# The last down product by Strassen's seven products, with weight sums added up in DRAM by accumulating DMAs

## The chip, the core and the metric

The kernel runs on one core of one Trainium2 chip. The metric is the device time of one execution in microseconds (us). A core has TensorE (PE in the profile; its weight loads are PEld), VectorE (DVE), ScalarE (ACT), GpSimd (POOL) and SyncE (SP), each with an instruction queue of its own that it works through in order, and 16 DMA engines that carry every transfer.

## The reference, cut to what matters

Two transformer blocks run one after the other on 512 tokens of width 1024. The change is in the last matrix product of the second block.

```python
D_MODEL = 1024
SEQ = 512
D_FF_2 = 2816

def second_block(x, ...):
    ...
        x = x + rmsnorm(y @ w_out[l], g_post_mix[l])
        h = rmsnorm(x, g_pre_ffn[l])
        gu = h @ w_ffn_in[l]
        gate, up = gu[..., :D_FF_2], gu[..., D_FF_2:]
        x = x + rmsnorm((jax.nn.silu(gate) * up) @ w_ffn_down[l], g_post_ffn[l])
    return x
```

The last product multiplies the hidden rows (512 tokens x 2816) by `w_ffn_down` (2816 x 1024). Its result is normalized per token, scaled by a gain, added to x, and is the output.

## The kernel before

All arithmetic is float32 at near full accuracy: each operand is split into a high part (a rounding CAST on ACT, line 93) and a low part (the difference, on DVE, line 98), and each product is three matmuls, high by high, high by low and low by high (`mm3`, `mm3s`, issued on line 109). A 128x128 block is the stationary operand, and up to 512 columns move past it.

Weights come through one stream, `Stream`. `_dma` (line 166) loads a tile of 128 partitions x 1024 columns (512 KB) into one of six `raw` buffers from SP's queue; `_split` makes its high and low parts in tiles `q`, of which there are 39. `next(key)` hands out the next pair and keeps up to `AHEAD` = 4 tiles split in advance. The order of the stream is written out beforehand, in `second_order` for the second block.

The order of instructions on each engine is not that of the Python code: the tile framework's scheduler places each instruction in its engine's queue by its dependences. `keep_in_program_order` pins a few of them.

The up products (gate and up, class `UpPairs`) already use seven products per pair of hidden tiles. `out` and `out_plain` leave each of the 22 hidden tiles (128 hidden x 512 tokens) in half a `q` tile, `gt(f)`.

`ffn_out` computes the last product. For every hidden tile f it splits `g[f]` once and takes one weight tile of 128 x 1024. For each of four token tiles t and two halves of the columns c it adds three matmuls 128x512 into one of eight PSUM banks: 22 x 4 x 2 x 3 = 528 matmuls. The last six hidden tiles are done token tile by token tile, so that the norm and the output of one token tile lie beside the products of the next:

```python
            k.mm3(ps[t][c], g[f][:, 0, t * P : (t + 1) * P], g[f][:, 1, t * P : (t + 1) * P],
                  w[0][:, c * 512 : (c + 1) * 512], w[1][:, c * 512 : (c + 1) * 512], f == 0, f == NF - 1)
```

One place at the program's start matters too. The first feed-forward block's norm is taken late: PE begins with products of the unnormalized x, and while they run, the sums of squares go through DVE (`nv`, line 317), through a power of -0.5 on POOL (`nr`, line 325), which is POOL's first arithmetic, back to DVE (line 332, a diagonal tile `b`) and to PE, which spreads them over all partitions by `ones` matmuls. The rows of this broadcast stand in PE's queue between two groups of products:

```python
    k.nc.gpsimd.tensor_tensor(out, in_, k.mhalf[:, :w], op=ALU.pow)
```

Of the kernel before, what the change touches and what calls it, by code (L numbers as in the profile page):

```python
# [8 lines left out]
F32 = mybir.dt.float32  # L9
# [6 lines left out]
P = 128  # L16
# [20 lines left out]
class Ctx:  # L37
    def __init__(self, ctx, tc, aps):
        self.tc = tc
        self.nc = tc.nc  # L40
        self.a = aps
        pool = lambda name, bufs, **kw: ctx.enter_context(tc.tile_pool(name=name, bufs=bufs, **kw))
        self.cp = pool("cp", 1)
        self.rawp = pool("raw", Stream.RAW)
        self.qp = pool("q", 39)
        self.bp = pool("b", 8)
        self.sp = pool("sm", 4)
        self.psp = pool("ps", 8, space=bass.MemoryType.PSUM)
# [373 lines left out]
class UpPairs:  # L422
# [125 lines left out]
    def run(self):  # L548
# [9 lines left out]
        for n, num in steps:  # L558
# [25 lines left out]
            if (n, num) == (NF // 2 - 1, 7):  # L584
                for f in range(2):
                    split_g(k, self.g, f)
# [1319 lines left out]
def tile_block(ctx: ExitStack, tc: tile.TileContext, aps, out):  # L1906
# [37 lines left out]
    second_order(W, aps)  # L1944
# [37 lines left out]

    M = Mixer(k)
# [11 lines left out]
    cat = [None] * KD  # L1995
    tq, tk, tg = M.ret_specs(rb)
# [4 lines left out]
    M.gates()  # L2001
    mem1 = Memory(k, aps["memT"], G["norm_mem_kv"])
# [3 lines left out]
    del mem1  # L2006
    xs, norm = [], Norm(k)
# [8 lines left out]
    run_all(weave(MA.q_stack(0), u, RATES["mq"]) or ())  # L2016
    k2d = dr.tile([4, P, 256], F32, name="k2d")
# [24 lines left out]
    del mem2  # L2042
    ops, norm = Operands(k), Norm(k)
# [24 lines left out]
    run_all(second_mix(k, G, x, xs, norm, norm5, k2d, v2d, dr, out))  # L2068


def second_order(W, a):
# [36 lines left out]
    for f in range(NF):  # L2108
        W.add(("down", f), a["w_ffn_down"][f])


def second_mix(k, G, x, xs, norm, norm5, k2d, v2d, dr, out):
# [36 lines left out]
    ns = Nsa(k, rt, rb)  # L2149
    u = units(k, [("T", ("q2", h), take_q2) for h in range(4)] + [("R", ("mlv", 0), ml.take_v)], xs, first)  # L2150
# [106 lines left out]
    def resid(h):  # L2257
        last = pns[h].finish()
        return lambda: resid2(h, last())
# [62 lines left out]
    up = UpPairs(k, ("gate", "up"), ops, finish, 6, lambda: resid(1))  # L2322
    g = up.run()
    gb = k.q([P, 2, S])
    nc.sync.dma_start(gb, k.a["g_post_rows"])
    ffn_out(k, "down", g, xtd, gb, e2, out)


def ffn_out(k, key, g, xtd, gb, e2, out):

    nc = k.nc
    last = 6
    ps = [[k.ps(), k.ps()] for t in range(NT)]

    def chunk(t, f, w, cs=(0, 1)):
        for c in cs:
            k.mm3(ps[t][c], g[f][:, 0, t * P : (t + 1) * P], g[f][:, 1, t * P : (t + 1) * P],
                  w[0][:, c * 512 : (c + 1) * 512], w[1][:, c * 512 : (c + 1) * 512], f == 0, f == NF - 1)  # L2340

    split_g(k, g, 0)
    for f in range(NF - last):
        split_g(k, g, f + 1)
        w = k.W.next((key, f))
        for t in range(NT):
            chunk(t, f, w)
    for f in range(NF - last + 1, NF):
        split_g(k, g, f)
    xt = []  # L2350
    for t in range(NT):
        xt.append(k.q([P, 2, S]))
        nc.sync.dma_start(xt[t], xtd[t])
    ws = [k.W.next((key, f)) for f in range(NF - last, NF)]
    for t in range(NT):
        for cs in ((0, 1),) if t < NT - 1 else ((0,), (1,)):
            for j, w in enumerate(ws):
                chunk(t, NF - last + j, w, cs)
        ss = k.small([P, 2], "os")
        ys = []  # L2360
        for c in range(2):
            sq, y = k.b(), k.b()
            nc.scalar.activation(sq, ps[t][c], AF.Square, scale=D**-0.5, accum_out=ss[:, c : c + 1])
            nc.vector.tensor_mul(y, ps[t][c], gb[:, c, :])
            ys.append(y)
        v = k.small([P, 1], "ov")
        nc.vector.scalar_tensor_tensor(v, ss[:, 0:1], e2[:, t : t + 1], ss[:, 1:2], op0=ALU.add, op1=ALU.add)  # L2367
        r = k.small([P, 1], "or")
        k.rsqrt(r, v)
        for c, y in enumerate(ys):  # L2370
            nc.vector.scalar_tensor_tensor(y, y, r, xt[t][:, c, :], op0=ALU.mult, op1=ALU.add)
            (nc.sync, nc.scalar)[c].dma_start(out[t][:, c * 512 : (c + 1) * 512], y)
# [56 lines left out]
def _host(inputs):  # L2429
# [38 lines left out]
    o["w_ffn_down"] = i["w_ffn_down_2"][0].reshape(NF, P, D)  # L2468
# [47 lines left out]
```

## Time and profile before

| what | value |
|---|---|
| time, median of 3 runs | 2206.36 us (2205.94 to 2207.67) |
| time of the profiled execution | 2205.79 us |
| its span, first to last instruction | 2204.0 us |
| PE busy | 2180.3 us (99%) |
| DVE busy | 1519.0 us (69%) |
| ACT busy | 1021.3 us (46%) |
| POOL busy | 307.8 us (14%) |
| granted TensorE clock, mean | 0.999 |

The profiled execution takes 1.8 us more than its span, for what lies around the instructions. Busy time counts the time in which an engine has an instruction under way; matmuls overlap, so that a row's mean duration is longer than the distance from one to the next.

### The profile page before, as it was taken

The numbers are of one execution on the slowest core, as the hardware profiler recorded it, in microseconds if no ns is written. First come the engines' busy times: TensorE is split into PE (matmuls) and PEld (weight loads), VectorE is DVE, ScalarE is ACT, GpSimd is POOL, SyncE is SP. The second block draws the span as 40 slices with busy tenths as digits, with TensorE's granted clock in tenths as the row PEclk, the third lists the DMA queues.
The fourth block names the chain that finished last, engine by engine and source line by source line (L and its number), as shares of the span: only waits on it lengthen the run. The fifth ranks groups of instructions, "written<-read, shape, count | busy, mean of one in ns | idle before, by whom it ended". The sixth has DMA issues, their size and how long they took to land.

```text
span 2204.0 us, 32737 instructions
## 1 busy us (share of the span) xinstructions
PE 2180.3 (99%) x12746; PEld 1902.9 (86%) x12746; DVE 1519.0 (69%) x2605; ACT 1021.3 (46%) x1794; POOL 307.8 (14%) x363
## 2 busy tenths in 40 slices
PE   9999999999999999999999999999999999999998
PEld 8999888888888889999888878887787789999987
DVE  7888644656866667888445955836888757888832
ACT  6545523545344544456324543315667636454620
POOL 0000022301234030000240000313334200000000
PEclk9999999999999999999999999999999999999999
DMA  5233524212333332335134122531111453133521
GB/s 177 96 116 108 183 64 136 79 61 86 124 125 106 106 115 77 115 106 188 55 116 149 54 92 97 185 138 59 48 59 55 131 169 116 61 113 106 166 102 39
DMA packets 78627, 235.73 MB, mean 107 GB/s; under 512 B 9092, under 2 KB 13444, under 8 KB 78472
## 3 DMA queue, kind: packets, MB, share of 16 engines
q1 hardware_dynamic: 75032, 226.12, 31.2%
q0 software_dynamic: 1280, 4.20, 0.5%
q10 hardware_dynamic: 2160, 3.32, 0.4%
q8 instruction: 100, 1.64, 0.3%
q14 instruction: 55, 0.45, 0.1%
HBM read 216.30 MB, written 17.30 MB: 106 GB/s over the span
## 4 chain that ended last, share of the span: by engine, by line
PE 85%; DVE 7%; ACT 3%; issue 2%; POOL 2%; DMA 1%; SPq 0%; POOLq 0%; DVEq 0%; ACTq 0%
PE ps L109 82%; PE ps L118 2%; DVE q L98 2%; ACT q L93 1%; DVE nx L1773 1%; ACT q L1775 1%; POOL hr L325 1%; DVE q L99 0%; DMA raw<-in_ffn_w_dram 0%; ACT b L285 0%; ACT q L1202 0%; DVE b L289 0%; POOL q L1606 0%; DVE q L2267 0%; POOL q L1780 0%
## 5 line engine op out<-in xcount | busy, mean ns | idle before, releaser
L109 PE MATMUL ps<-q,q 128*128 128x512 f32 (+3 forms) x11736 | 2106.4, 340 | 5.1 <-ACT b L464 3.1
L109 PEld LDWEIGHTS ps<-q,q 128*128 128x128 f32 x11736 | 1795.0, 190 | 235.7 <-issue 6.6
L98 DVE TENSOR_TENSOR q<-raw,q 128x1024 fp32r<-128x1024 f32 (+3 forms) x389 | 430.6, 1123 | 114.1 <-ACT q L93 70.5
L93 ACT CAST q<-raw 128x1024 fp32r<-128x1024 f32 (+3 forms) x389 | 351.1, 931 | 107.3 <-PE ps L109 74.5
L98 DVE TENSOR_TENSOR q<-q,q 128x1024 fp32r<-128x1024 f32 (+1 forms) x188 | 189.9, 1029 | 60.7 <-ACT q L93 53.3
L93 ACT CAST q<-q 128x1024 fp32r<-128x1024 f32 (+1 forms) x188 | 164.8, 893 | 136.9 <-PE ps L109 68.8
L473 ACT ACTIVATE b<-b 128x256 f32<-128x256 f32 x108 | 44.9, 417 | 136.1 <-DVE b L472 136.1
L1775 ACT ACTIVATE q<-ps,nx 128x128 f32<-128x128 f32 (+3 forms) x128 | 67.4, 531 | 57.0 <-DVE nx L1773 26.1
L1780 POOL TENSOR_SCALAR q<-q,nr 128x128 f32<-128x128 f32 (+3 forms) x128 | 72.0, 569 | 143.0 <-DVE nr L1778 98.7
L118 PE MATMUL ps<-ident,q 128*128 128x128 f32 x512 | 81.5, 274 | 7.8 <-POOL q L1780 2.5
L464 ACT COPY b<-ps 128x512 f32<-128x512 f32 x81 | 47.3, 584 | 83.4 <-PE ps L109 83.4
L118 PEld LDWEIGHTS ps<-ident,q 128*128 128x128 f32 x512 | 61.9, 140 | 25.8 <-POOL q L1780 8.0
L98 DVE TENSOR_TENSOR q<-ps,q 128x512 fp32r<-128x512 f32 x112 | 74.4, 683 | 11.2 <-ACT q L93 10.8
L296 POOL TENSOR_TENSOR b<-q 128x512 f32<-128x512 f32 x32 | 36.9, 1156 | 312.2 <-DVE q L1980 108.6
L94 ACT ACTIVATE q<-q,gains 128x512 fp32r<-128x512 f32 (+1 forms) x48 | 30.5, 648 | 105.2 <-DVE q L1980 34.6
L300 POOL TENSOR_TENSOR b<-b,b 128x512 f32<-128x512 f32 (+1 forms) x49 | 70.7, 1447 | 2.8
L93 ACT CAST q<-ps 128x512 fp32r<-128x512 f32 x112 | 62.9, 593 | 17.2 <-PE ps L109 12.0
L1773 DVE TENSOR_REDUCE nx<-ps 128x1 f32<-128x384 f32 (+3 forms) x96 | 56.1, 584 | 0.0
L99 DVE SCALAR_TENSOR_TENSOR q<-q,gains,q 128x512 fp32r<-128x512 f32 (+1 forms) x48 | 35.6, 754 | 20.2 <-ACT q L94 19.8
L325 POOL TENSOR_TENSOR sr<-ss,mhalf 128x4 f32<-128x4 f32 x8 | 8.1, 1006 | 293.5 <-DVE ss L1405 186.0
L325 POOL TENSOR_TENSOR or<-ov,mhalf 128x1 f32<-128x1 f32 x4 | 2.2, 546 | 324.2 <-DVE ov L2367 324.2
L474 DVE TENSOR_TENSOR q<-b,b 128x256 f32<-128x256 f32 x81 | 34.1, 424 | 19.2 <-ACT b L473 19.0
(266 smaller groups left out, 1437.8 us busy)
## 6 DMA issues: line engine op xcount, KB each, us to landing
raw<-in_ffn_w_dram SPq DMA_DIRECT2D x100, 512.0 KB, 4.3
raw<-in_w_ffn_in_dram SPq DMA_DIRECT2D x44, 512.0 KB, 3.7
raw<-in_w_gm_dram SPq DMA_DIRECT2D x24, 512.0 KB, 3.3
raw<-in_ffn_w2a_dram SPq DMA_DIRECT2D x22, 512.0 KB, 4.9
raw<-in_w_ffn_down_dram SPq DMA_DIRECT2D x22, 512.0 KB, 4.4
raw<-in_w_out_dram SPq DMA_DIRECT2D x16, 512.0 KB, 3.3
raw<-in_w_mk_dram SPq DMA_DIRECT2D x8, 512.0 KB, 3.7
raw<-in_w_mv_dram SPq DMA_DIRECT2D x8, 512.0 KB, 3.8
```

Of the source, the lines that this page charges most:

```text
L93: return self.nc.scalar.copy(out, in_)
L98: return self.nc.vector.tensor_sub(out, in_, hi.bitcast(F32))
L99: return self.nc.vector.scalar_tensor_tensor(out, in_, gain, hi.bitcast(F32), op0=ALU.mult, op1=ALU.subtract)
L109: return self.nc.tensor.matmul(out, a, b, start=start, stop=stop, skip_group_check=skip)
L118: return self.nc.tensor.transpose(out, in_, self.ident[:n, :n])
L296: k.nc.gpsimd.tensor_tensor(t, x, x, op=ALU.mult)
L300: k.nc.gpsimd.tensor_tensor(self.acc, self.acc, t, op=ALU.add)
L464: self.k.nc.scalar.copy(z, bank)
L473: nc.scalar.activation(t, t, AF.Silu)
L1773: nc.vector.tensor_reduce(mx, s.rearrange("p j b t -> p b j t"), axis=AX.XY, op=ALU.max, negate=True)
L1775: nc.scalar.activation(pr[b][:, :n], s[:, :, c, :], AF.Exp, bias=mx[:, c : c + 1], accum_out=sm[:, c : c + 1])
L1780: nc.gpsimd.tensor_scalar(pr[b][:, :n], pr[b][:, :n], r[:, c : c + 1], 1.0, op0=ALU.mult, op1=ALU.mult)
```

## The change

The product is computed as seven products of quarter size. The hidden dimension is split by even and odd hidden tiles, the tokens by even and odd token tiles (rows r), and the 1024 columns into two halves. Seven products `num`, in the order 1, 2, 6, 5, 7, 3, 4, each take 11 hidden tiles by two token tiles (q) by 512 columns: 7 x 11 x 2 x 3 = 462 matmuls of 128x512. Their results are added up on DVE (`take`).

Each of the seven has a token operand of its own, made by adding and subtracting quarters of the hidden rows on DVE (`HiddenRows.sums`, `operand`) and split again, and a weight operand of its own, 128 x 5632 floats, read in five tiles of 1024 columns and one of 512 (m = 0 to 5). Three of the weight operands are quarters of `w_ffn_down`; four are sums of quarters, t1 to t4. The sums are made on the device by DMAs in DRAM (`DownSums.step`): for each of the four, a copy of 2.88 MB (5632 x 128 floats) into a DRAM tile and then an accumulating DMA of the same size onto it. t2 starts from t1, and t4 from t2. The eight DMAs are written one by one at eight `sums.step()` calls, between the first block's stages and at the start of the second. They are issued from POOL's queue. The accumulating ones are cut into pieces of 512 bytes (`max_dma_last_dim=S`).

The core of the diff:

```diff
@@ second_order
-    for f in range(NF):
-        W.add(("down", f), a["w_ffn_down"][f])
+    for n, num in enumerate(DownSums.STEPS):
+        for m in range(DownSums.NM):
+            W.add(("down", num, m), sums.source(num, m))
...
+class DownSums:
+    NM = (NF // 2 + 1) // 2
+    STEPS = (1, 2, 6, 5, 7, 3, 4)
+
+    def __init__(self, k, w, dr):
+        self.k = k
+        b = {(e + 1, c + 1): w[e, c] for e in range(2) for c in range(2)}
+        t = {n: dr.tile([P, NF // 2 * S], F32, name=f"t{n}d") for n in (1, 2, 3, 4)}
+        self.src = {1: b[1, 1], 2: b[2, 1], 3: b[2, 2], 4: t[4], 5: t[1], 6: t[2], 7: t[3]}
+        self.todo = [(t[1], b[1, 1], False), (t[1], b[1, 2], True), (t[2], t[1], False), (t[2], b[2, 2], True),
+                     (t[3], b[1, 2], False), (t[3], b[2, 2], True), (t[4], t[2], False), (t[4], b[2, 1], True)]
+
+    def step(self):
+        if self.todo:
+            dst, src, add = self.todo.pop(0)
+            rows = lambda v: v.rearrange("p (n c) -> (p n) c", c=S)
+            if add:
+                self.k.nc.gpsimd.dma_start(rows(dst), rows(src), accum_op=ALU.add, max_dma_last_dim=S)
+            else:
+                self.k.nc.gpsimd.dma_start(rows(dst), rows(src))
...
+    def operand(self, num, m):
+        if (num, m) in self.split:
+            return self.split.pop((num, m))
+        k, nc = self.k, self.k.nc
+        if num == 6:
+            a11 = self.part(0, m, 0)
+            nc.vector.scalar_tensor_tensor(a11, self.s1[m], -1.0, a11, op0=ALU.mult, op1=ALU.subtract)
+        src = self.s1[m] if num == 5 else self.part(*{1: (0, m, 0), 2: (1, m, 0), 6: (0, m, 0), 7: (0, m, 1), 3: (1, m, 0), 4: (1, m, 1)}[num])
+        n = src.shape[1]
+        t = k.q([P, 2, 4, P], F32R)
+        k.split(t[:, 0, :n], t[:, 1, :n], src)
+        return t
...
+    def chunk(num, m, a, w, qs=(0, 1)):
+        b = {5: "y", 3: "y", 2: "z"}.get(num, "x")
+        for j in range(w[0].shape[1] // S):
+            for q in qs:
+                if num in (1, 2, 5) and m == 0 and j == 0:
+                    bank[b, q] = k.ps()
+                i, c = 2 * j + q, slice(j * S, (j + 1) * S)
+                k.mm3s(bank[b, q], a[:, 0, i], a[:, 1, i], w[0][:, c], w[1][:, c],
+                       num in (1, 2, 5) and m == 0 and j == 0, 2 * m + j == NF // 2 - 1)
...
+    for n, (num, m) in enumerate(items):
+        if n + 1 < len(items):
+            ready[items[n + 1]] = rows.operand(*items[n + 1])
+        rows.sums(num, m)
...
+        w = k.W.next((key, num, m))
+        a = ready.pop((num, m))
+        if num == 4 and m >= late:
+            held.append((m, a, w))
+            continue
+        chunk(num, m, a, w)
+        if m == NM - 1:
+            for q in range(2):
+                take(num, q)
```

The change moves instructions in two places that the prediction speaks of. The first is the head of POOL's queue, at the program's start. Before, it reads as follows; `mhalf` is the constant of the power, `nr` the first norm's power of -0.5, and the DMAs after it reload x for the second stage. A DMA's shape is rows x elements of four bytes; in brackets stand the semaphores that an instruction waits for.

```order
L2511 UNCONDITIONAL_BRANCH [waits barrier_Pool_Activation_PE_DVE_SP_gather]
L1914 MEMSET mhalf 128x16
L325 ISA
L325 TENSOR_TENSOR nr_459<-nv_457,mhalf 128x4 [waits DVE_49,Pool_49]
L1975 DMA q_2787<-in_xT_dram 128x512 [waits DVE_49,PE_49]
```

In the changed program it reads:

```order
L1916 MEMSET mhalf 128x16
L2365 DMA t1d<-in_w_ffn_down_dram 64x11264
L2365 DMA t3d<-in_w_ffn_down_dram 64x11264
L2363 DMA t1d<-in_w_ffn_down_dram 5632x128 [waits DMASW0_49]
L2363 DMA t3d<-in_w_ffn_down_dram 5632x128 [waits DMASW1_49]
L2365 DMA t2d<-t1d 64x11264 [waits DMASW2_49]
L2363 DMA t2d<-in_w_ffn_down_dram 5632x128 [waits DMASW4_49]
L2365 DMA t4d<-t2d 64x11264 [waits DMASW5_49]
L2363 DMA t4d<-in_w_ffn_down_dram 5632x128 [waits DMASW6_49]
L325 ISA
L325 TENSOR_TENSOR nr_463<-nv_461,mhalf 128x4 [waits DVE_49,Pool_49]
L1978 DMA q_2791<-in_xT_dram 128x512 [waits DVE_49,PE_49]
```

All eight DMAs of `DownSums.step`, wherever their calls stand in the code, now stand ahead of `nr`, and six of them wait for the completion (DMASW) of an earlier one of the eight. The rest of POOL's queue is as before.

The second place is DVE's queue at the start of the last product. Before, the low part of a hidden tile (512 columns) and that of a weight tile (1024 columns) take turns, one pair for each 24 matmuls:

```order
L98 TENSOR_TENSOR q_20578<-q_18242,q_20578 128x512
L98 TENSOR_TENSOR q_20582<-raw_20540,q_20581 128x1024
L98 TENSOR_TENSOR q_20611<-q_18315,q_20611 128x512
L98 TENSOR_TENSOR q_20615<-raw_20546,q_20614 128x1024
L98 TENSOR_TENSOR q_20644<-q_18315,q_20644 128x512
```

In the changed program, where line 2415 is a difference of quarters of the hidden rows for a later product and line 2419 one in place:

```order
L98 TENSOR_TENSOR q_20577<-q_18887,q_20577 128x512
L2415 TENSOR_TENSOR q_20580<-q_18504,q_18393 128x512
L2415 TENSOR_TENSOR q_20580<-q_18998,q_18887 128x512
L98 TENSOR_TENSOR q_20583<-raw_20549,q_20582 128x512
L2419 TENSOR_TENSOR q_18393<-q_18393 128x4x128
L98 TENSOR_TENSOR q_20600<-q_19381,q_20600 128x512
L98 TENSOR_TENSOR q_20605<-raw_20555,q_20604 128x1024
```

One operand, one weight tile and now a sum go with each 12 matmuls.

## Rows read from the trace of the kernel before

**Rows 1.** The page: busy time by engine, and PE's row by 40 slices.

```profile
span 2204.0 us, 32737 instructions
PE 2180.3 (99%) x12746; PEld 1902.9 (86%) x12746; DVE 1519.0 (69%) x2605; ACT 1021.3 (46%) x1794; POOL 307.8 (14%) x363
PE   9999999999999999999999999999999999999998
```

**Rows 2.** PE's groups from 2071 us to the end: count, busy us, mean ns.

```profile
L109 PE MATMUL ps<-q,q 128*128 128x512 f32 x528 | 119.9, 389 | 0.0
```

**Rows 3.** DVE's low parts in the last product, in order of time: start, us.

```profile
2083.94 0.69 DVE L98 TENSOR_TENSOR q<-q,q 128x512 fp32r<-128x512 f32 x1
2084.54 1.22 DVE L98 TENSOR_TENSOR q<-raw,q 128x1024 fp32r<-128x1024 f32 x1
2085.68 0.69 DVE L98 TENSOR_TENSOR q<-q,q 128x512 fp32r<-128x512 f32 x1
```

**Rows 4.** Windows of the last product: busy us (x), PE's clock, DMA share, GB/s.

```profile
core 0: us, PE busy (x) PEld busy (x) DVE busy (x) ACT busy (x) POOL busy (x), PEclk, DMA share, GB/s
2080.00:2100.00 20.00, 20.00 (x90) 16.57 (x89) 19.60 (x23) 16.02 (x23) 0.00 (x0) 1.00 0.86 299
2100.00:2120.00 20.00, 20.00 (x90) 16.55 (x89) 8.24 (x10) 6.96 (x9) 0.00 (x0) 1.00 0.24 78
```

**Rows 5.** All engines around POOL's first power, in order of time; in brackets idle time.

```profile
35.70 5.75 PE L109 MATMUL ps<-q,q 128*128 128x512 f32 x24
...
39.69 0.15 DVE L317 TENSOR_SCALAR nv<-ps 128x4 f32<-128x4 f32 x1
...
39.99 1.02 POOL L325 TENSOR_TENSOR nr<-nv,mhalf 128x4 f32<-128x4 f32 x1 [39.14 <-DVE nv L317]
41.05 0.87 DVE L332 TENSOR_SCALAR b<-ident,nr 128x128 f32<-128x128 f32 x4 [1.21 <-POOL nr L325]
41.45 0.97 PEld L109 LDWEIGHTS ps<-b,ones 128*128 128x128 f32 x8 [0.43 <-PE ps L109]
41.48 1.13 PE L109 MATMUL ps<-b,ones 128*128 128x128 f32 x8
...
42.37 19.89 PE L109 MATMUL ps<-q,q 128*128 128x512 f32 x121
```

**Rows 6.** POOL's groups over the span: its DMA instructions, busy us, mean ns, idle before.

```profile
L1975 POOL DMA_DIRECT2D q<-in_xT_dram x8 | 4.5, 566 | 188.3 <-PE ps L109 188.3
```

**Rows 7.** DMA queues from 0 to 32 us: packets, MB, share of 16 engines.

```profile
q1 hardware_dynamic: 5526, 8.72, 82.1%
q10 hardware_dynamic: 432, 0.18, 2.3%
```

**Rows 8.** DMA queues from 225 to 240 us, where POOL's own loads run.

```profile
q0 software_dynamic: 516, 1.73, 30.1%
```

**Rows 9.** The page's DMA issues: KB each, us from issue to landing.

```profile
x3d<-q ACTq DMA_DIRECT2D x8, 256.0 KB, 2.0
raw<-in_w_ffn_down_dram SPq DMA_DIRECT2D x22, 512.0 KB, 4.4
```

**Rows 10.** Windows after PE's short stops in the first stage.

```profile
60.00:70.00 10.00, 7.64 (x55) 7.43 (x55) 8.97 (x12) 4.35 (x7) 0.00 (x0) 0.89 0.16 54
70.00:80.00 10.00, 10.00 (x80) 10.00 (x80) 10.00 (x15) 5.48 (x7) 0.00 (x0) 0.94 0.63 210
80.00:90.00 10.00, 10.00 (x86) 10.00 (x85) 7.64 (x14) 4.66 (x8) 0.00 (x0) 1.00 0.01 2
```

**Rows 11.** The last token tile, in order of time from PE's last product.

```profile
2197.01 0.60 ACT L2363 ACTIVATE b<-ps 128x512 f32<-128x512 f32 x1 [3.33 <-PE ps L109]
...
2199.21 1.42 DVE L2371 SCALAR_TENSOR_TENSOR b<-b,or,q 128x512 f32<-128x512 f32 x2 [0.66 <-POOL or L325]
```

More of the change, by code (lines that the diff above doesn't have):

```diff
@@ L584, in run @@
             if (n, num) == (NF // 2 - 1, 7):
-                for f in range(2):
+                if self.rows is not None:
+                    self.rows.early()
+                for f in range(2) if self.rows is None else ():
                     split_g(k, self.g, f)
@@ L1981, in tile_block @@
         next_x(k, x, xs, d, G["norm_mix"][:, d : d + 1], norm)
+    sums.step()
     M = Mixer(k)
@@ L1995, in tile_block @@
     cat = [None] * KD
+    sums.step()
     tq, tk, tg = M.ret_specs(rb)
@@ L2001, in tile_block @@
     M.gates()
+    sums.step()
     mem1 = Memory(k, aps["memT"], G["norm_mem_kv"])
@@ L2006, in tile_block @@
     del mem1
+    sums.step()
     xs, norm = [], Norm(k)
@@ L2016, in tile_block @@
     run_all(weave(MA.q_stack(0), u, RATES["mq"]) or ())
+    sums.step()
     k2d = dr.tile([4, P, 256], F32, name="k2d")
@@ L2042, in tile_block @@
     del mem2
+    sums.step()
     ops, norm = Operands(k), Norm(k)
@@ L2057, in tile_block @@
         nc.gpsimd.dma_start(x[d], x3d[d])
+    sums.step()
     gc = k.const([P, KD], "gc")
@@ L2149, in second_mix @@
     ns = Nsa(k, rt, rb)
+    sums.step()
     u = units(k, [("T", ("q2", h), take_q2) for h in range(4)] + [("R", ("mlv", 0), ml.take_v)], xs, first)
@@ L2320, in finish @@
         return second
[L2322 to L2329, printed above, removed]
-    nc = k.nc
[L2334 to L2365, printed above, removed]
@@ new lines, in second_mix, with source @@
+    rows_ = HiddenRows(k)
+    up = UpPairs(k, ("gate", "up"), ops, finish, 6, lambda: resid(1), rows_)
+    up.run()
+    del up
+    ffn_out(k, "down", rows_, xtd, e2, out)
+class DownSums:
[16 more added lines that the diff above has]
+                self.k.nc.gpsimd.dma_start(rows(dst), rows(src))
+    def source(self, num, m):
+        return self.src[num][:, 2 * m * S : min(2 * m + 2, NF // 2) * S]
@@ new lines, in ffn_out, with square, gain, tile_out @@
+def ffn_out(k, key, rows, xtd, e2, out):
+    nc = k.nc
+    NM, steps = DownSums.NM, DownSums.STEPS
+    late = NM - 3
+    bank = {}
+    c1, c2, c4, xt = [], [], [], []
+    ss = [k.small([P, 2], "os") for _ in range(NT)]
+    def chunk(num, m, a, w, qs=(0, 1)):
[7 more added lines that the diff above has]
+                       num in (1, 2, 5) and m == 0 and j == 0, 2 * m + j == NF // 2 - 1)
+    def square(t, c, v):
+        nc.scalar.activation(k.b(), v, AF.Square, scale=D**-0.5, accum_out=ss[t][:, c : c + 1])
+    def gain(c, dst, v):
+        if c == 0:
+            nc.vector.tensor_mul(dst, v, gb[:, 0, :])
+        else:
+            nc.vector.scalar_tensor_tensor(dst, v, -1.0, gb[:, 1, :], op0=ALU.mult, op1=ALU.mult)
+    def tile_out(t, ys):
@@ L2371, in ffn_out, with take @@
             nc.vector.scalar_tensor_tensor(y, y, r, xt[t][:, c, :], op0=ALU.mult, op1=ALU.add)
-            (nc.sync, nc.scalar)[c].dma_start(out[t][:, c * 512 : (c + 1) * 512], y)
+            (nc.sync, nc.scalar)[c].dma_start(out[t][:, c * S : (c + 1) * S], y)
+    def take(num, q):
+        if num in (1, 6, 5):
+            t = k.half()
+            nc.scalar.copy(t, bank["y" if num == 5 else "x", q])
+            {1: c1, 6: c2, 5: c4}[num].append(t)
+        if num == 2:
+            nc.vector.tensor_add(c1[q], c1[q], bank.pop(("z", q)))
+            square(2 * q, 0, c1[q])
+            gain(0, c1[q], c1[q])
+        if num == 7:
+            nc.vector.tensor_add(c4[q], c4[q], bank["x", q])
+            square(2 * q + 1, 1, c4[q])
+            gain(1, c4[q], c4[q])
+        if num == 3:
+            nc.vector.tensor_add(c2[q], c2[q], bank.pop(("y", q)))
+            square(2 * q, 1, c2[q])
+            gain(1, c2[q], c2[q])
+            tile_out(2 * q, (c1[q], c2[q]))
+        if num == 4:
+            p, y = bank.pop(("x", q)), k.b()
+            square(2 * q + 1, 0, p)
+            gain(0, y, p)
+            tile_out(2 * q + 1, (y, c4[q]))
+    items = [(num, m) for num in steps for m in range(NM)]
+    ready = {items[0]: rows.operand(*items[0])}
+    gb = k.q([P, 2, S])
+    nc.sync.dma_start(gb, k.a["g_post_rows"])
+    held = []
+    for n, (num, m) in enumerate(items):
+        if n + 1 < len(items):
+            ready[items[n + 1]] = rows.operand(*items[n + 1])
+        rows.sums(num, m)
+        if num == 3 and m < NT:
+            xt.append(k.q([P, 2, S]))
+            nc.sync.dma_start(xt[m], xtd[m])
+        w = k.W.next((key, num, m))
[7 more added lines that the diff above has]
+                take(num, q)
+    for q in range(2):
+        for m, a, w in held:
+            chunk(4, m, a, w, (q,))
+        take(4, q)
 def weave2(main, fill, rate):
```

51 lines of the change are left out of this document (42 added, 9 removed).

## Prediction

> **What bounds the kernel now.** I read the page first: PE is busy 99% of the span, in every slice but the last [rows 1]. So PE's own work and whatever makes PE wait are the time; DVE, ACT, POOL and the DMA engines count only where they hold PE up. Then I read the stage that is changed. From 2071 us to the end PE has 528 matmuls of 128x512, 119.9 us busy, with no idle time before them [rows 2]: 119.9 / 528 = 0.227 us each. The mean of 0.389 us in that row is the length of one with its overlap and is not used. After the first 20 us of the stage DVE and ACT are idle more than half the time and the DMA share falls to 0.24 [rows 4]: nothing but PE limits the product before.
>
> The order of the changed program sends me to a second place, the program's start, since eight DMAs now stand ahead of POOL's first power `nr`. There I read all engines in order of time [rows 5]. DVE delivers the sums `nv` at 39.69; POOL, idle for 39.14 us, makes `nr` at 39.99 to 41.01; DVE makes the diagonal `b` from 41.05; PE ends its products at 41.45 and takes up the `ones` matmuls at 41.48. PE waits 0.03 us. The reader is to see that this chain has no slack: the first piece of `b` and PE's last product before it end within 0.1 us of each other. Everything behind the broadcast in PE's queue (the 121 products from 42.37) waits for it, and so does DVE's queue behind line 332. Each microsecond by which `nr` is late is a microsecond of PE.
>
> **The change, part by part.**
>
> *Matmuls.* 528 become 462, of the same shape and in the same kind of run: 66 x 0.227 = **-15.0 us**.
>
> *DVE in the last product.* Its starts lie 0.60 us apart for 512 columns and 1.14 for 1024 [rows 3]. Weights: 7 x 11 x 512 columns x 0.57 = 43.9 us; operands 38.5 x 0.60 = 23.1; the sums of quarters, four rounds of 5.5, at some 0.65 = 14.3; the 12 additions and gains of `take` some 8. That is about 89 us beside 462 x 0.227 = 104.9 of PE. DVE does not become the bound on average, but at the start of the stage, and when a product ends and DVE must wait for PE before it adds, PE may catch it up. One step of PE is 12 x 0.227 = 2.7 us; the work that DVE has queued after the second product (two additions, two gains, three in-place sums, a weight tile) is about 5.8 us against an advance of two steps. I take **+2 us**, between 0 and 10. ACT needs 0.95 and 0.52 us per step by the same kind of reckoning and stays under 65 us.
>
> *Weight loads.* 512 KB per 2.7 us is 193 GB/s; in the window where the stream caught up, 299 GB/s were moved [rows 4], and six buffers cover 16 us beside a landing of 4.4 us [rows 9]. Nothing for that; if the cover went, xtd's 2 MB in product 3 would cost up to 7 us.
>
> *The end.* After the last matmul stand the same square, power, scaling and store [rows 11]: nothing.
>
> *The eight DMAs on POOL.* This is the term that decides. Six of the eight wait for an earlier one to land, they stand in POOL's queue, and `nr` stands behind all of them. Only t3's pair is independent; the rest is one chain: copy t1, add t1, copy t2, add t2, copy t4, add t4 issued. So I build up when POOL is through.
>
> A copy is 2.88 MB. POOL's own loads moved 1.73 MB with 30.1% of 16 engines in 15 us [rows 8]: 72.2 us of engine time, 41.7 us per MB, so 7.5 us for a copy on 16 engines. At the start the weight queue itself takes 82.1% of the engines for 32 us [rows 7]; with equal shares a copy takes 15 us there. A landing costs some 2.0 us more, the time of a 256 KB store to DRAM from issue to landing [rows 9], taken whole.
>
> An accumulate is 5632 pieces of 512 bytes, 352 for each engine. No row shows one. On the engines, small packets of ACT's queue took 2.3% of 16 x 32 us for 432 packets of some 420 bytes [rows 7]: 27 ns each. 352 of them take 9.6 us, and 19.2 us if the destination is read like the source. That is the lower bound. On POOL, a DMA instruction of 128 rows took 0.566 us [rows 6]. If all of that goes with the rows, 5632 rows take 24.9 us; if none of it does, 0.6. I take **24.9 us**, POOL's part in proportion to the rows, since that is the only row on what a DMA costs POOL, and hold that the engines move the pieces meanwhile. The upper bound is that POOL's part and the moving follow each other, 24.9 + 19.2 = 44.1 us, or more if the pieces wait for each other (below).
>
> The Trainium skill, "DMA: Bandwidth & Descriptors", section "Anatomy of one DMA — SWDGE (gpsimd) path", calls the generation of descriptors small and says that many can be emitted before an incremental cost shows. By it an accumulate is bound by the engines, and the sum would be the first rival's. The trace has DMAs of 128 rows alone on POOL and can't tell.
>
> Then, in us from the start: copy t1 issued at 0.9, done 15.0 later, landed at 17.9. Add t1 holds POOL to 42.8, add t3 to 67.7 (t3's copy landed long before). Copy t2 goes out at 67.7 and lands at 77.2. Add t2 holds POOL to 102.1 and lands at 104.1. Copy t4 lands at 113.6. Add t4 holds POOL to 138.5. Then `nr` runs, 98.5 us later than at 39.99: **+98.5 us**. The weights at the start, which the copies delay by up to 15 us, lie under this stall and cost nothing more.
>
> *The clock.* After PE's short stops between 60 and 70 us the granted clock was 0.89 and 0.94 in two windows of 10 us before it was 1.00 again [rows 10]: 1.7 us of work lost. I take the same, **+1.7 us**, after the long stop.
>
> Sum, on the profiled execution: 2205.8 - 15.0 + 2.0 + 98.5 + 1.7 = **2293 us**. The median of the runs is 0.6 us above the profiled execution, which changes nothing.
>
> **The rivals.**
>
> *POOL's part is a fixed price, the engines set the pace.* With 19.2 us for an accumulate and the two first copies through at about 33: add t1 to 52, add t3 to 71.5, copy t2 landed at 81, add t2 at 102.2, copy t4 at 111.7, POOL free at 112.3. `nr` is 72.3 us late: **2267 us**. For it: nothing shows that POOL's 0.566 us grows with the rows. With 9.6 us instead, POOL is free at 83.4: **2238 us**.
>
> *POOL's part, then the moving.* With 44.1 us in series: add t1 to 62.0, add t3 to 86.9, copy t2 landed at 96.4, add t2 at 142.5, copy t4 at 152, POOL free at 176.9: **2331 us**.
>
> *Accumulates that wait for themselves.* If an engine had one piece under way at a time at the 2.0 us of a landing, an accumulate would take 704 us and the kernel twice its time; with 16 under way, 44 us. Nothing in the trace says how many. From 60 us on each, the time is above **2385 us**.
>
> *POOL's arithmetic is not held up.* If the waiting DMAs did not hold `nr`, or all eight were through by 53 us, the kernel would gain: 2205.8 - 13.0 = 2193 us, plus up to 15 for a start in which the copies take engines that are 82.1% busy: some **2200 us**. For it: in [rows 6] the DMA that held POOL for 188.3 us had nothing ready behind it, so blocking is not seen. Against it: the queue is one, and the bytes alone (seven transfers of at least 7.5 us and four landings of 2.0) exceed 53 us. It decides at a delay of 13 us.
>
> *The product saves little.* If DVE held PE up by the whole 10 us, the time would be 2301, inside the forecast's own spread.
>
> **How the numbers follow.** The forecast has 0.40, the fixed price 0.25 at 19.2 us and 0.06 at 9.6, the two in series 0.15, the slow accumulates 0.10, no hold-up 0.04. The range of 2245 to 2385 leaves out 2238 and less (0.10) and the slow ones (0.10). The forecast's own range is 2280 to 2310. A measurement of this kernel can tell about 0.2% (4.4 us) from no change. Faster by more than that only where POOL isn't held up, 0.04; within it 0.01; slower 0.95.
>
> **What the profile after would show.** Right: POOL's row `nr` starts near 139 instead of 39.99, ended by nothing but its own queue, PE idle from about 41 to 140 with the `ones` matmuls waiting for DVE and POOL, and then the old sequence some 99 us later; in the last product 462 matmuls in about 105 to 110 us with DVE near 85% busy; the clock under 1.00 for 20 us after the stop. Wrong: `nr` near 40 with PE running on, which would mean that the waits don't hold POOL; or POOL's DMA rows of about 0.6 us with long waits between them, which would mean that the engines, not POOL's part, set the pace; or a last product longer than 115 us, with PE's idle time ended by DVE or by `raw` loads.

## The result and the profile after

The changed kernel takes 2286.6 us, median of four runs (2283.8 to 2288.2), beside 2207.0 us for the kernel before in the same session: a ratio of 1.036, 95% interval 1.035 to 1.037. The profiled execution took 2283.8 us, its span 2282.0 us at a mean granted clock of 0.979. The forecast was 2293 us. The time is near it and the sign is right; the way to it was partly another, which POOL's rows show.

The page of the changed kernel, PE's busy time, its row by 40 slices and its granted clock:

```profile
PE 2170.0 (95%) x12680; PEld 1892.1 (83%) x12680; DVE 1566.8 (69%) x2675; ACT 1050.4 (46%) x1840; POOL 325.4 (14%) x371
...
PE   6169999999999999999999999999999999999998
...
PEclk7679999999999999999999999999999999999999
```

Where [rows 1] had a 9 in every slice but the last, the first three slices of 57 us each now have 6, 1 and 6. Everything that was lost was lost there. POOL in the changed kernel, in order of time, from its first DMA to the first norm's power (start, us, what; in brackets the idle time and what ended it):

```profile
1.31 0.75 POOL L2365 DMA_DIRECT2D t1d<-in_w_ffn_down_dram  x1 [0.46 <-issue]
2.05 0.54 POOL L2365 DMA_DIRECT2D t3d<-in_w_ffn_down_dram  x1
14.98 3.77 POOL L2363 DMA_DIRECT2D t1d<-in_w_ffn_down_dram  x1 [12.39 <-DMA t1d<-in_w_ffn_down_dram]
65.64 3.71 POOL L2363 DMA_DIRECT2D t3d<-in_w_ffn_down_dram  x1 [46.90 <-issue]
67.63 2.26 POOL L2365 DMA_DIRECT2D t2d<-t1d  x1
95.53 3.69 POOL L2363 DMA_DIRECT2D t2d<-in_w_ffn_down_dram  x1 [25.64 <-DMA t2d<-t1d]
117.52 0.52 POOL L2365 DMA_DIRECT2D t4d<-t2d  x1 [18.30 <-DMA t2d<-in_w_ffn_down_dram]
129.05 3.69 POOL L2363 DMA_DIRECT2D t4d<-in_w_ffn_down_dram  x1 [11.01 <-DMA t4d<-t2d]
131.14 2.77 POOL L325 TENSOR_TENSOR nr<-nv,mhalf 128x4 f32<-128x4 f32 x1
```

`nr` starts at 131.14 instead of 39.99 [rows 5], 91.2 us late. Its row begins inside that of the last accumulate and is 2.77 us long instead of 1.02, so it ends at 133.91 instead of 41.01, 92.9 us late. But an accumulate (line 2363) holds POOL for 3.7 us, not for the 24.9 of the forecast, and what fills the time between is waiting: for a copy or an accumulate to land, and once for something the profile doesn't name: t3's accumulate goes out 46.9 us behind the row before it, though the copy that it waits for had landed at about 23.8.

PE in order of time around the stall, with DVE's row that feeds it:

```profile
59.24 5.75 PE L109 MATMUL ps<-q,q 128*128 128x512 f32 x24
134.38 2.04 PE L109 MATMUL ps<-b,ones 128*128 128x128 f32 x8 [69.39 <-DVE b L332]
```

```profile
133.94 0.88 DVE L332 TENSOR_SCALAR b<-ident,nr 128x128 f32<-128x128 f32 x4 [67.36 <-POOL nr L325]
```

PE's products before the broadcast end at 64.99 instead of 41.45 [rows 5], and PE then waits 69.4 us for the diagonal, which waits for `nr`: 23.5 and 69.4 us are the 92.9 by which PE's `ones` matmuls are late (134.38 instead of 41.48). Three windows at the end of the stall (busy us, count, granted clock, DMA share, GB/s):

```profile
120.00:130.00 10.00, 0.00 (x0) 0.00 (x0) 0.00 (x0) 0.00 (x0) 0.95 (x1) 0.50 0.62 216
130.00:140.00 10.00, 5.62 (x21) 4.88 (x22) 4.87 (x10) 2.49 (x4) 3.91 (x2) 0.58 0.90 110
140.00:150.00 10.00, 10.00 (x53) 8.60 (x52) 9.97 (x16) 6.41 (x8) 0.00 (x0) 1.00 1.42 180
```

The clock is at its lower level while PE stands still, 0.58 in the window in which PE takes up work, and 1.00 in the next.

The last product, by shape from 2150 us to the end, and its windows:

```profile
L109 PE MATMUL ps<-q,q 128*128 128x512 f32 x462 | 105.6, 390 | 0.1
```

```profile
2172.00:2192.00 20.00, 19.90 (x86) 15.79 (x85) 20.00 (x30) 14.49 (x23) 0.00 (x0) 1.00 0.72 218
2192.00:2212.00 20.00, 20.00 (x89) 16.52 (x88) 19.99 (x29) 11.73 (x19) 0.00 (x0) 1.00 0.61 195
...
sum 100.00, PE 99.90 PEld 82.01 DVE 86.17 ACT 60.50 POOL 1.49; mean PE 19.98 PEld 16.40 DVE 17.23 ACT 12.10 POOL 0.30
```

It is 105.6 us beside the 119.9 of [rows 2], 14.3 us less, with 0.1 us of idle time. DVE is busy 86 of these 100 us and full in the first 40, yet PE hardly waits for it.

The account nearly closes. PE takes up the broadcast 92.9 us late; at the next stage, where POOL reloads x, 91.4 us of it are left (before, then after the change; the part on the clock below has the difference):

```profile
229.29 4.48 POOL L1975 DMA_DIRECT2D q<-in_xT_dram  x8 [188.28 <-PE ps L109]
```

```profile
320.69 4.39 POOL L1978 DMA_DIRECT2D q<-in_xT_dram  x8 [186.78 <-PE ps L109]
```

91.4 less 14.3 us are 77.1 us; the spans differ by 78.0. The remaining 0.9 us is not accounted for.

### The profile page after: what moved, and what is told of

It reads as the page before. It is cut to its first block, busy times and chain, and to the rows that moved or that the text cites. A ratio compares the mean times of both kernels' runs of the same rounds, so it can differ in the third digit from the quotient of the medians.

```text
span 2282.0 us, 32826 instructions
## 1 busy us (share of the span) xinstructions
PE 2170.0 (95%) x12680; PEld 1892.1 (83%) x12680; DVE 1566.8 (69%) x2675; ACT 1050.4 (46%) x1840; POOL 325.4 (14%) x371
## 4 chain that ended last, share of the span: by engine, by line
PE 81%; DVE 7%; issue 4%; DMA 4%; ACT 2%; POOL 2%; POOLq 0%; DVEq 0%; SPq 0%; ACTq 0%
PE ps L109 79%; PE ps L118 2%; DVE q L98 2%; DMA t2d<-t1d 1%; DMA t3d<-in_w_ffn_down_dram 1%; DMA t2d<-in_w_ffn_down_dram 1%; ACT q L1777 1%; DVE nx L1775 1%; POOL hr L325 1%; DMA t4d<-t2d 0%; ACT q L93 0%; DVE q L99 0%; DVE b L289 0%; ACT q L1204 0%; POOL q L1608 0%
## 5 line engine op out<-in xcount | busy, mean ns | idle before, releaser
L109 PE MATMUL ps<-q,q 128*128 128x512 f32 (+3 forms) x11670 | 2095.8, 340 | 23.2 <-ACT q L94 20.2
L98 DVE TENSOR_TENSOR q<-raw,q 128x1024 fp32r<-128x1024 f32 (+3 forms) x409 | 451.8, 1119 | 126.5 <-ACT q L93 85.6
L93 ACT CAST q<-raw 128x1024 fp32r<-128x1024 f32 (+3 forms) x409 | 369.4, 929 | 118.7 <-PE ps L109 62.8
L93 ACT CAST q<-q 128x1024 fp32r<-128x1024 f32 (+1 forms) x208 | 175.9, 859 | 199.7 <-DVE q L384 87.0
L98 DVE TENSOR_TENSOR q<-q,q 128x1024 fp32r<-128x1024 f32 (+1 forms) x208 | 201.8, 985 | 58.6 <-ACT q L93 49.3
L118 PEld LDWEIGHTS ps<-ident,q 128*128 128x128 f32 x512 | 61.8, 140 | 25.9 <-POOL q L1782 8.0
L109 PE MATMUL ps<-b,ones 128*128 128x128 f32 x72 | 11.0, 294 | 69.9 <-DVE b L332 69.9
L109 PEld LDWEIGHTS ps<-b,ones 128*128 128x128 f32 x72 | 10.1, 207 | 71.0 <-issue 69.8
```

The lines of the kernel that those rows point to most:

```text
L93: return self.nc.scalar.copy(out, in_)
L98: return self.nc.vector.tensor_sub(out, in_, hi.bitcast(F32))
L109: return self.nc.tensor.matmul(out, a, b, start=start, stop=stop, skip_group_check=skip)
L118: return self.nc.tensor.transpose(out, in_, self.ident[:n, :n])
```

## Experiments

The first question was whether all the loss is POOL's queue at the start (theory A), or whether the 23 MB of the eight transfers cost PE wherever they run (theory B).

**Pinned.** All eight stay in POOL's queue where their calls are written.

```diff
-                self.k.nc.gpsimd.dma_start(rows(dst), rows(src), accum_op=ALU.add, max_dma_last_dim=S)
+                d = self.k.nc.gpsimd.dma_start(rows(dst), rows(src), accum_op=ALU.add, max_dma_last_dim=S)
             else:
-                self.k.nc.gpsimd.dma_start(rows(dst), rows(src))
+                d = self.k.nc.gpsimd.dma_start(rows(dst), rows(src))
+            self.k.tc.keep_in_program_order(d)
```

> The changed kernel with each of the eight DMAs pinned in POOL's queue where its call is written, so that none stands ahead of the first power. If the loss is POOL's queue standing ahead of that power (theory A), all of the 91 us comes back and the 14.3 us of the product stay: 2207.0 - 14.3 = 2193 us, between 2191 and 2197. If the DMAs' traffic costs PE time wherever it runs (theory B), PE loses again what it lost to late weights at the start, some 20 us spread over the eight places: 2205 to 2215.

Measured: 2202.9 us, ratio 0.998 (0.997 to 0.999). 84 us are gone, so the loss lay at the start; what of it the waits in the queue make, and what the transfers themselves, the last kernel below asks. But the time lies between the two theories, some 10 us above A.

**Without the sums.** The changed kernel without the eight DMAs; the four summed operands are replaced by quarters of the weights.

```diff
-        self.src = {1: b[1, 1], 2: b[2, 1], 3: b[2, 2], 4: t[4], 5: t[1], 6: t[2], 7: t[3]}
...
+        self.src = {1: b[1, 1], 2: b[2, 1], 3: b[2, 2], 4: b[2, 1], 5: b[1, 1], 6: b[1, 2], 7: b[2, 2]}
+        self.todo = []
```

> The changed kernel without the eight DMAs: the four summed weight operands are replaced by quarters of the matrix as they lie there, so that the last product computes something else with the same instructions. This is the price of the seven products by themselves. From the profile after: 528 matmuls in 119.9 us became 462 in 105.6, so 2207.0 - 14.3 = 2193 us under theory A and theory B alike; what a run with the sums in another place has above this is the price of the sums.

Measured: 2191.9 us, ratio 0.994 (0.992 to 0.995): the seven products are worth 14.4 us by the medians, as the profile said.

**The sums alone.** The kernel before with the same eight DMAs at the head of POOL's queue, their results unused.

```diff
+    sums_only(k, aps["w_ffn_down"], dr)
...
+    for dst, src, add in todo:
+        if add:
+            k.nc.gpsimd.dma_start(dst, src, accum_op=ALU.add, max_dma_last_dim=S)
+        else:
+            k.nc.gpsimd.dma_start(dst, src)
```

> The kernel before with the same eight DMAs at the head of POOL's queue (the sums are of other pieces of the same size and are not used). Theory A: the first power at about 131 us and everything after it 91 us later, 2207 + 91 = 2298 us. If part of the 91 us came from something in the seven products or from the other order of instructions, less than 2290.

Measured: 2299.1 us (one run), 92.8 above the kernel before, with `nr` at 131.62. The two parts add up: +92.8 - 14.4 = +78.4, beside +79.6 by the medians of the whole change.

**Longer pieces.** What sets the pace of the eight: POOL's work for each piece, or the engines?

```diff
-                self.k.nc.gpsimd.dma_start(rows(dst), rows(src), accum_op=ALU.add, max_dma_last_dim=S)
+                self.k.nc.gpsimd.dma_start(rows(dst), rows(src), accum_op=ALU.add, max_dma_last_dim=4 * S)
```

> The changed kernel with the accumulating DMAs cut into pieces of 2048 bytes instead of 512: 88 pieces for each engine instead of 352. The profile after shows 64 ns for a piece of 512 bytes and 21.7 us for an accumulate. If the engines' price goes by bytes with a fixed part for each piece, as for plain packets (27 ns for some 420 bytes, 140 ns for 3.35 KB), read twice, a piece takes about 0.16 us and an accumulate about 16 us; and if the wait of 46.9 us ahead of the second accumulate (until the first had landed) comes from the number of pieces that can be queued, it is gone. Then POOL is free at about 95 us instead of 131 and the time is about 2250 us. If an accumulate is bound by bytes alone and the second one waits all the same, 2280 to 2287 us.

Measured: 2262.9 us (one run), 24 less, but not the 2250 that was expected. POOL in this kernel, in order of time, the rows of the accumulates and of t2's copy:

```profile
14.59 1.57 POOL L2363 DMA_DIRECT2D t1d<-in_w_ffn_down_dram  x1 [12.01 <-DMA t1d<-in_w_ffn_down_dram]
23.84 1.49 POOL L2363 DMA_DIRECT2D t3d<-in_w_ffn_down_dram  x1 [7.68 <-DMA t3d<-in_w_ffn_down_dram]
42.33 0.53 POOL L2365 DMA_DIRECT2D t2d<-t1d  x1 [16.99 <-DMA t1d<-in_w_ffn_down_dram]
69.58 1.48 POOL L2363 DMA_DIRECT2D t2d<-in_w_ffn_down_dram  x1 [26.72 <-DMA t2d<-t1d]
...
110.53 1.48 POOL L2363 DMA_DIRECT2D t4d<-in_w_ffn_down_dram  x1 [10.63 <-DMA t4d<-t2d]
```

POOL's part falls from 3.7 to 1.5 us for a quarter of the pieces, which gives back 2.2 us each and can't be the 20 us by which `nr` is earlier (111.51). They come from t1's accumulate, which lands 27.4 us after its issue instead of 50.4: t2's copy waits for it, and goes out at 42.33 instead of 67.63. Some of that is lost again, since t2's accumulate takes 29.5 us to land instead of 21.7. So the engines set the pace, not POOL's work.

The wait of 46.9 us is gone too: t3's accumulate goes out at 23.84, as soon as its copy has landed, while t1's is still under way. But that gains little. With the wait or without it, t2's copy stands behind t1's accumulate and runs beside t3's; it takes 27.4 us with the wait and 27.0 here. The next two kernels ask what that wait was.

**Half the rows, and pieces of 1024 bytes.**

```diff
-                self.k.nc.gpsimd.dma_start(rows(dst), rows(src), accum_op=ALU.add, max_dma_last_dim=S)
+                self.k.nc.gpsimd.dma_start(rows(dst)[: 64 * (NF // 2)], rows(src)[: 64 * (NF // 2)], accum_op=ALU.add, max_dma_last_dim=S)
```

> The changed kernel with its eight transfers at the head of POOL's queue, but each accumulate covers only the first half of its rows (2816 pieces of 512 bytes; t1 to t4 are then only partly sums). It asks why t3's accumulate waited 46.9 us until t1's had landed, a wait without a releaser in the profile. Theory X (the number of pieces queued at once: 5632 fit, as one accumulate shows, 11264 don't): the two accumulates have 5632 together, so t3's goes out as soon as its copy has landed, near 24 us. Rival Y (pieces of 512 bytes, or two accumulates of them, wait for each other): t3's accumulate waits for t1's, 20 us or more without a releaser. POOL's part should be about 2.2 us, and an accumulate should land in 11 to 12 us where nothing else runs. The power nr at 75 to 95 us, the time 2232 to 2250 us.

```diff
-                self.k.nc.gpsimd.dma_start(rows(dst), rows(src), accum_op=ALU.add, max_dma_last_dim=S)
+                self.k.nc.gpsimd.dma_start(rows(dst), rows(src), accum_op=ALU.add, max_dma_last_dim=2 * S)
```

> The changed kernel with pieces of 1024 bytes, 2816 for a whole accumulate. Theory X: again 5632 pieces for two accumulates, so t3's goes out near 24 us, right after its copy. Rival Y of another kind (the bytes that wait, 2 x 2.88 MB): excluded already by the pieces of 2048 bytes, so only a limit between 2816 and 5632 pieces would make it wait. POOL's part should be about 2.2 us. The power nr between 111 us (pieces of 2048 bytes) and 131 us (512), the time 2262 to 2284 us.

Measured: 2252.0 and 2272.4 us (one run each). The row of t3's accumulate in the first and in the second:

```profile
24.29 2.23 POOL L2363 DMA_DIRECT2D t3d<-in_w_ffn_down_dram  x1 [7.17 <-DMA t3d<-in_w_ffn_down_dram]
```

```profile
23.98 2.22 POOL L2363 DMA_DIRECT2D t3d<-in_w_ffn_down_dram  x1 [5.85 <-DMA t3d<-in_w_ffn_down_dram]
```

Both go out with their copy. So the wait comes neither with the 512 bytes (which the first has) nor with the 2.88 MB (which the second has): it comes with the number of pieces queued at once, 5632 in both of these and 11264 in the changed kernel. `nr` is at 98.91 and 119.14. The first was expected at 75 to 95 us and 2232 to 2250, and is a little later; its half accumulates land in 12.5 us where little else runs. The second lies in its range. In both, t2's copy goes out with the landing of t1's accumulate, at 41.73 and 49.02.

**Where the pinned version loses.** Its PE waits (in all, times, longest) hold two rows that the version without the sums has not, or has at 0.5 us for the second at this place:

```profile
PE ps L109 <- POOL b L300: 4.6, 1, 4.6
...
PE ps L109 <- DVE b L332: 2.8, 1, 2.8
```

POOL in the pinned version at the two places, in order of time:

```profile
542.42 0.58 POOL L2365 DMA_DIRECT2D t2d<-t1d  x1
...
555.71 1.45 POOL L296 TENSOR_TENSOR b<-b 128x256 f32<-128x256 f32 x2 [4.57 <-DMA b<-in_memT_dram]
```

```profile
1162.49 3.74 POOL L2363 DMA_DIRECT2D t4d<-in_w_ffn_down_dram  x1
1164.52 2.79 POOL L325 TENSOR_TENSOR r<-nv,mhalf 128x4 f32<-128x4 f32 x1
```

The first: a load that POOL's additions need lands late behind the copy of t2, and the sum of squares that PE needs next is late. The second: a power of another norm stands right behind t4's accumulate. Without the sums it took 1.03 us:

```profile
1160.53 1.03 POOL L325 TENSOR_TENSOR r<-nv,mhalf 128x4 f32<-128x4 f32 x1 [1.36 <-DVE nv L2132]
```

After each of the two stops the granted clock falls, in the pinned version:

```profile
560.00:570.00 10.00, 10.00 (x47) 8.00 (x48) 6.60 (x12) 4.16 (x5) 0.71 (x1) 0.77 0.35 99
...
1170.00:1180.00 10.00, 10.00 (x41) 8.69 (x41) 7.52 (x16) 2.63 (x4) 0.00 (x0) 0.72 1.39 191
```

4.6 + 2.3 us of waits, and 2.3 + 2.8 us of PE's work in these two windows, are 12.0 us, beside the 11.0 between the medians. That is theory C: not the traffic wherever it runs, but two places. The two traces, laid side by side, show the same. From POOL's power at 541.46 (543.92 without the sums) to the one at 575.15 (570.08) the pinned version takes 7.5 us longer, and from the addition at 1157.56 (1154.20) to the power at 1342.61 (1334.00) 5.2 us. Elsewhere it is 2.5 us ahead (up to the first of these rows), 1.7 ahead (between the two places) and 0.5 behind (to the end). The next two kernels test theory C.

**A quiet stretch.** All eight, pinned, taken from their eight places and put right behind the second norm's power of the other up products.

```diff
-    sums.step()
...
-    up = UpPairs(k, ("ffn2_w1", "ffn2_w3"), ops, lambda norm=norm: norm.finish(None, k.rb))
+    def finish(norm=norm):
+        last = norm.finish(None, k.rb)
+        while sums.todo:
+            sums.step()
+        return last
+
+    up = UpPairs(k, ("ffn2_w1", "ffn2_w3"), ops, finish)
...
```

> All eight transfers one after the other right behind the second power nr of the up products (at 828 us), a stretch of 198 us in which POOL has no arithmetic and the weight stream takes 0.32 of the DMA engines. Theory C (the 11 us that the pinned version loses against the version without the sums are two places: a load that POOL's additions wait for 4.6 us behind the t2 copy at 542 us, and a power that waits behind the 3.7 us of t4's accumulate at 1162 us, each with a drop of the clock after it): nothing waits for POOL or for a late load here, so the time is that without the sums, 2193 us (2191 to 2196). Theory B (the 23 MB cost PE some 1.4 us a transfer wherever they run): 2200 to 2206 us, as in the pinned version. In both the eight are through before 1026 us, some 150 us for the chain.

Measured: 2193.2 us (2191.3 to 2195.4, five runs) beside 2206.6, ratio 0.994 (0.992 to 0.995): the time without the sums, 2191.9, within the spread. Theory B falls: here the 23 MB cost nothing that can be measured. Some of POOL's rows (line 2363 is the copy here and 2361 the accumulate), and two windows of the stretch:

```profile
823.58 0.59 POOL L2363 DMA_DIRECT2D t1d<-in_w_ffn_down_dram  x1
835.62 3.77 POOL L2361 DMA_DIRECT2D t1d<-in_w_ffn_down_dram  x1 [11.45 <-DMA t1d<-in_w_ffn_down_dram]
861.48 0.52 POOL L2363 DMA_DIRECT2D t2d<-t1d  x1 [22.09 <-DMA t1d<-in_w_ffn_down_dram]
...
946.12 3.69 POOL L2361 DMA_DIRECT2D t4d<-in_w_ffn_down_dram  x1 [32.01 <-DVE q L217]
```

```profile
870.00:910.00 40.00, 40.00 (x336) 40.00 (x335) 35.45 (x55) 19.72 (x30) 4.33 (x3) 1.00 1.12 268
910.00:950.00 40.00, 40.00 (x335) 40.00 (x335) 35.36 (x55) 19.68 (x29) 7.80 (x3) 1.00 1.12 270
```

POOL's eight rows reach over 122.5 us, about as long as at the start (127.7), but no arithmetic stands behind them for 198 us. The DMA engines are full, and PE is busy in all of both windows at full clock. (The last row's releaser is the profile's inference; the copy of t4 that it waits for lands at about 945.7.)

**Small copies.** The pinned version with its copies in pieces of 2048 bytes instead of 45056: was the late load held by long pieces?

```diff
-                d = self.k.nc.gpsimd.dma_start(rows(dst), rows(src))
+                d = self.k.nc.gpsimd.dma_start(rows(dst), rows(src), max_dma_last_dim=4 * S)
```

> The pinned version with the four copies cut into pieces of 2048 bytes instead of 45056. Theory C1 (the load that POOL waited for behind the t2 copy was late because the engines were held by long pieces): the wait of 4.6 us at 551 us is under 1 us, the drop of the clock after it is gone, and the time is about 5 us below that of the pinned version, 2197 us. Rival C2 (the load was late because of the 2.88 MB that stood ahead, in whatever pieces): the wait stays at 3 to 6 us and the time at 2202 us. POOL's part of a copy should be about 1.5 us instead of 0.55, as for an accumulate of as many pieces.

Measured: 2201.2 us (one run). The same row of POOL:

```profile
556.31 1.45 POOL L296 TENSOR_TENSOR b<-b 128x256 f32<-128x256 f32 x2 [4.88 <-DMA b<-in_memT_dram]
```

The load is as late as before: long pieces are not the reason, and C1 falls. C2, the 2.88 MB ahead of it, stands. POOL's part of the copy was 0.96 us, less than the 1.5 expected. At the second place PE's wait is as long as in the pinned version (2.9 beside 2.8 us), but the clock behind it stays at 1.00 here, and the place costs 2.4 us instead of 5.2 (from the addition at 1157.95 to the power at 1340.16, beside the version without the sums). The window behind it:

```profile
1170.00:1180.00 10.00, 10.00 (x52) 8.61 (x53) 9.24 (x19) 2.64 (x4) 0.00 (x0) 1.00 1.33 190
```

So the clock's part of theory C came with this stop in one execution and not in the other.

**Two copies first.** The quiet version, but with the copies of t1 and t3 at the head of POOL's queue as in the changed kernel: what do they cost where no wait stands in the queue?

```diff
+    sums.step()
+    sums.step()
...
-        self.todo = [(t[1], b[1, 1], False), (t[1], b[1, 2], True), (t[2], t[1], False), (t[2], b[2, 2], True),
+        self.todo = [(t[1], b[1, 1], False), (t[3], b[1, 2], False), (t[1], b[1, 2], True), (t[2], t[1], False),
...
+            if len(self.todo) < 6:
+                self.k.tc.keep_in_program_order(d)
```

> Only the copies of t1 and t3, which wait for nothing, stand ahead of the first power nr; the other six transfers run in the quiet stretch at 828 us. It prices the start's weight loads, which the forecast held to be late by up to 15 us and hidden under POOL's stall. Theory A: the queue holds nr up by waits alone, so nr follows nv at once; PE's products before the broadcast end some 15 us late (two copies of 7.5 us engine time), and the time is 2193 + 15 + 2 for the clock = 2210 us (2205 to 2219, the upper end if the 23.5 us seen in the changed kernel come from the copies alone). Rival: the loads share the engines and nothing is late, 2193 to 2197 us; then the stall hid nothing.

Measured: 2210.0 us (one run), 16.8 above the quiet version. POOL's power:

```profile
57.96 1.04 POOL L325 TENSOR_TENSOR nr<-nv,mhalf 128x4 f32<-128x4 f32 x1 [55.40 <-DVE nv L317]
```

It follows DVE's `nv` and nothing holds it in its queue, but it is 18.0 us later than in [rows 5], and PE reaches the broadcast 20.2 us later (61.65 beside 41.48) without waiting for it. The loads of PE's first products share the 16 engines with 5.8 MB. The smallest of them land 20.6 us after their issue instead of 2.8 (this kernel, then the kernel before):

```profile
raw<-in_ffn_w_dram SPq DMA_DIRECT2D x6, 64.0 KB, 20.6
```

```profile
raw<-in_ffn_w_dram SPq DMA_DIRECT2D x6, 64.0 KB, 2.8
```

At POOL's first reload of x, 16.8 us are left (245.77 beside 229.00 in the quiet version), as in the time. The Trainium skill, "DMA: Bandwidth & Descriptors", section "Issuing engines are not separate DMA queues", says that transfers run on the same 16 engines whichever engine starts them; the 20.6 us of these loads, which SP issues beside POOL's copies, agree.

## Why the prediction was right, and where its steps were not

*That `nr` stands behind all eight and PE behind `nr`.* Right, and it is the loss: +92.8 us by the sums alone, none of it that can be measured left in the quiet stretch.

*The +98.5 us.* Measured 92.9, at the end of `nr` and at PE. The step that failed inside it is "I take 24.9 us, POOL's part in proportion to the rows". POOL's part is 3.7 us for 5632 pieces, 2.2 for 2816 and 1.5 for 1408, so about 0.7 us and 0.5 us for each 1000 pieces. The engines set the pace, as the first rival had it, and POOL's short rows with long waits between them are one of the signs of being wrong that the prediction named. The rule that the prediction weighed from the Trainium skill, "DMA: Bandwidth & Descriptors", section "Anatomy of one DMA — SWDGE (gpsimd) path", that generating descriptors is small, agrees with these rows, 3.7 us beside 21.7 to landing, though 3.7 us is enough to hold up a power that stands behind it. The landing agrees with the upper of the engine bounds: 19.2 us with the destination read too, and the 2.0 of a landing, are 21.2; the accumulates of t2 and t4 took 21.7 from issue to landing:

```profile
t2d<-t1d POOLq DMA_DIRECT2D x1, 2816.0 KB, 27.4
t2d<-in_w_ffn_down_dram POOLq DMA_DIRECT2D x1, 2816.0 KB, 21.7
t4d<-t2d POOLq DMA_DIRECT2D x1, 2816.0 KB, 11.1
t4d<-in_w_ffn_down_dram POOLq DMA_DIRECT2D x1, 2816.0 KB, 21.7
```

*Why the rival's 2267 was still too short.* It had the pace right and missed how the transfers share the engines. The first accumulate, beside the weight loads and t3's copy, took 50.4 us to land, the longest of t1's transfers:

```profile
DMA to landing us min/median/max: 2.5/4.5/50.4
```

So it landed at about 65.4 instead of the rival's 52. Even so t2's copy went out at 67.63, before the rival's 71.5: it needs t1's accumulate landed, and of t3's only POOL's part. But it then ran beside t3's accumulate and took 27.4 us instead of 9.5, so that t2's accumulate went out 14.5 us later than the rival's 81. The rest of the 18.8 us between its 112.3 and the 131.14 of `nr` are 0.8 us on t2's accumulate, 2.0 on t4's copy and 1.5 on POOL's part of t4's accumulate.

*Why the forecast came near all the same.* It had t2's copy go out at 67.7, and it went out at 67.63. That is a coincidence: the forecast had two accumulates of 24.9 us on POOL there, and the run had one that took 50.4 us to land and one that took 2.0 us of POOL before the copy. From there the copy of t2 took 18.3 us more than forecast (95.5 beside 77.2), the accumulate of t2 gave 4.9 of it back, the copy of t4 lost 2.0, so that t4's accumulate went out at 129.05 instead of 113.6, and that accumulate with `nr` behind it took 4.9 us instead of 25.9. Together that is 5.6 us less than forecast, and a sum that was near for partly wrong reasons.

*Copies of 7.5 us and 2.0 of landing.* The one copy that ran alone, t4's, took 11.1 us, 1.6 too low. The first one took at most 13.7 us (1.31 to 14.98), where the forecast had 17.0. For the copy of t2 the forecast had no other transfer on the engines, and that was the larger miss.

*Weight loads at the start "cost nothing more".* Right in this kernel: PE was 23.5 us late at 64.99 and stood until 134 anyway. Without the stall the two copies alone cost 16.8 us, so the rival that put a kernel without hold-up at some 2200 us belongs at 2210 or more.

*The seven products, -15.0 and +2.0.* Measured -14.3 in the profile and -14.4 in the timed runs: the term for DVE's lag was 2.0 and measures 0.7 (105.6 beside 104.9).

*The clock, +1.7.* Not even the sign came out. From the `ones` matmuls to the next group of products PE takes 25.90 us in both kernels (41.48 to 67.38 and 134.38 to 160.28). Its matmuls behind the stall are 1.9 us slower, but its wait ahead of that next group is 1.9 us shorter (before, then after):

```profile
67.38 2.83 PE L109 MATMUL ps<-q,q 128*128 128x256 f32 x13 [2.36 <-ACT b L464]
```

```profile
160.28 1.93 PE L109 MATMUL ps<-q,q 128*128 128x256 f32 x14 [0.48 <-ACT b L464]
```

The granted clock of 0.89 and 0.94 around the longer wait [rows 10] has no counterpart after the change, where it is 1.00 in all windows from 140 to 180 us. So 92.9 us late became 91.4, and the term is about -1.5. The forecast of 20 us at a lower clock after the stall was wrong too: it was full again from 140 us.

## What to carry to other kernels

A DMA that waits for another DMA is a stop sign in its engine's queue: before it is put there, look up which arithmetic stands behind it, who waits for that, and let the order of the queue, not the order of the code, answer. The same eight transfers cost 93 us at the head of POOL's queue, 11 us spread over places picked by the code's order, and nothing measurable in a stretch where POOL has no arithmetic and the loads have room. And a forecast that comes out near the time is worth taking apart: here an accumulate nearly seven times too dear on POOL (24.9 for 3.7 us) nearly cancelled against a slow first one and a copy that had to share the engines (27.4 for 9.5 us).

## What the runs showed of the hardware

An accumulating DMA from POOL, DRAM to DRAM, 2.88 MB in pieces of 512 bytes: 3.7 us of POOL and 21.7 us to land, about twice a plain copy (11.1). Beside other transfers it took longer: 25.6 to 28.8 us in the quiet stretch, 50.4 at the start. Half of it landed in 12.5 us, so about 52 ns for each piece on an engine, (21.7 - 12.5) / 176. Longer pieces help POOL but the landing little: 19.4 us (t4's) with 1024 bytes and 17.8 with 2048, where t2's took 29.5; why that one was slower stays open.

A DMA on POOL waits, without a releaser in the profile, when the pieces queued ahead of it and its own are too many: 5632 went out at once, 11264 did not. Where between the two the limit lies was not measured, and the wait added little to the time here.

The row of POOL's next arithmetic begins before the DMA's row ends (`nr` at 131.14, 2.1 us into a row of 3.69), but it is then 2.77 us long instead of 1.02. It ends 1.17 us after the DMA's row, and so it does with pieces of 2048 and 1024 bytes and with half the rows: the arithmetic gains nothing by the overlap.
